# Attention stages with only TensorE held to the written order, and constants set up ahead of an up chunk

## The chip, the cores and the metric

The kernel runs on one core of one Trainium2 chip. The metric is the device time of one execution in microseconds (us), taken as the median over runs. The engines are named as in the profile: PE is TensorE's matmuls, PEld its weight loads, DVE is VectorE, ACT is ScalarE, POOL is GpSimd, SP is SyncE, which issues most DMAs (SPq is its queue). L12 is line 12 of the kernel's source.

## The reference, cut to what matters

One sequence of 256 tokens of width 1024 goes through two stacks of two layers each. All arithmetic is fp32.

```
for l in range(2):                                     # first stack
    x = x + 0.5 * swiglu(rms_norm(x, g1[l]), ...)
    x = x + hybrid_mixer(rms_norm(x, gm[l]), ...)      # NSA (compressed + selected + window) and MoBA heads
    x = x + 0.5 * swiglu(rms_norm(x, g2[l]), ...)
x = rms_norm(x, norm_final)
for l in range(2):                                     # second stack
    h = rms_norm(x, attn_norm[l]);  proj = h @ w_in[l]
    ya = sparse_attention(...)      # 8 heads, each query keeps 64 keys chosen by an index score
    yb = rms_norm(diff_attention(...), b_subln[l])     # 4 heads: softmax 1 - lambda * softmax 2
    x = x + (sigmoid(g_a) * (ya @ w_up_a) + sigmoid(g_b) * (yb @ w_up_b)) @ w_out[l]
    x = x + (silu(h2 @ w_gate) * (h2 @ w_up)) @ w_ffn_out[l]
```

## The kernel before

**Stages.** The program is ten stages in a row: FFN, mixer, FFN, FFN, mixer, FFN (the first stack), then hybrid, FFN, hybrid, FFN. In the profiled execution the mixers run from 204 to 384 us and from 759 to 941 us, the hybrids from 1128 to 1371 us and from 1556 to 1793 us. Here they are called the four attention stages.

**Weights.** A full fp32 product is made of three passes over rounded halves: hi by hi, hi by lo, lo by hi. So every block of weights that lands from a DMA in a buffer `raw` is split in two steps: ACT copies it to `hi` (L189 in the FFN, L1586 in the attention stages), then DVE subtracts to make `lo` (L190, L1587). A half block is 128x1024. There are 3 `raw`, 4 `hi` and 4 `lo` buffers, and 4 accumulator banks `acc` in PSUM beside the banks `psS` (two), `psT` and `psO` (one each).

**Attention stages.** The big products of such a stage (projections L210 to L212, output or up projections) are work that can be put anywhere. A planner (`Fill`, L1595ff) lays them out in program order between the steps of the attention: `fill.us(t)` puts t us of matmuls there, and with them, in program text, the splits of weights that come next (`Fill.split`, by the progress of the product that is running). The attention itself is a row of slots (12 in a mixer, 8 in a hybrid, `pipeline`). In each slot PE makes the scores of two heads (L429 to L433). For each of the two heads and two blocks of queries DVE takes the negative maximum `nm` (L437) and ACT the exponential `P` (L440). DVE forms a coefficient `c` (L640 and L641, L634 with a gate; L1184 in a hybrid) and scales P by it (L479, L480). PE transposes P (L452, L453, L458), ACT copies the greater part of it out of PSUM as `PT` (L454), DVE the rest (L459), and PE multiplies it with the values (L494, L496; L1286 for differential heads). ACT and DVE then split the output (`oh`, `ol`; L223, L224). A slot's own fill lies between the transposes and the values, the scores of the next slot between those.

Other places of the mixer that matter here: `kt`, the transposed keys of the second kind (copied by DVE, L625), ahead of the scores of slot 1; the compressed branch's probabilities, also on DVE ahead of that (L890 to L903); the compression of keys and values, whose weights `ck` and `cv` are fetched by SP (L175, L800) and multiplied at L811; its GELU chain (L834 to L837) ahead of L842 and L858. In a hybrid the rope norm (DVE L1009, which needs POOL's L1002 and its root `hr`, L204) comes ahead of the first slot; the gates `ma` are made by DVE (L1215) and ACT (L1221).

**What sets the order.** From L707 in the mixer and L1375 in the hybrid a stage is under `tc.manual_schedule(engines=MANUAL)`, until its last slot and product are written. Engines in MANUAL execute in the order of the program text there. Elsewhere, and on engines outside MANUAL, a scheduler at build time picks from what is ready, and takes what stands first in the text.

**The first stage.** `ffn` runs over chunks c of 512 columns (L334): gate product, its evacuation (`total`, L327) and SiLU into `sgs`, then up product, whose banks come from psS, psT and psO, and its evacuation. In the first FFN alone a function `extra` makes constants (PE L138, L141, L960 into three acc banks, DVE `gcol` L139 and others behind them, then sine and cosine tables for the second stack). It is bound by `issue_after` to come after the latest product and weight split.

Of the kernel before, what the change touches and what calls it, by code (L numbers as in the profile page):

```python
# [14 lines left out]
ALU = mybir.AluOpType  # L15
AX = mybir.AxisListType
ENG = mybir.EngineType
MANUAL = {ENG.PE, ENG.Activation, ENG.DVE, ENG.Pool}
PSUM = bass.MemoryType.PSUM

DEPTH = 2
# [13 lines left out]
class K:  # L35
# [256 lines left out]
    def ffn(self, pr, wg, wu, wd, scale, after, start=None, load=None, extra=None):  # L292
        nc, tc = self.nc, self.tc
        xx = pr.xx
        self.n_ft = -1
        with tc.tile_pool(name="ffn", bufs=2) as fp:
            gh = fp.tile([128, NF, S], F32R, name="gh", bufs=1)
            gl = fp.tile([128, NF, S], F32R, name="gl", bufs=1)

            def product(w, c, n, banks, first):  # L300

                cs = slice(c * 512, c * 512 + n * 128)
                for h in range(2):
                    src = w[h * 512 : (h + 1) * 512, cs].rearrange("(k p) f -> p k f", p=128)
                    if first and h == 0:
                        hi, lo = start(lambda: self.weights(src, [4, n * 128], 2))
                    else:
                        hi, lo = self.weights(src, [4, n * 128])
                    for j in range(n):
                        fs = slice(j * 128, (j + 1) * 128)  # L310
                        for k in range(4):
                            xk = xx[:, 4 * h + k]
                            nc.tensor.matmul(  # L313
                                banks[j], hi[:, k, fs], xk.rearrange("p u s -> p (u s)"),
                                start=h == 0 and k == 0, stop=False,
                            )
                            self.last = nc.tensor.matmul(  # L317
                                banks[j][:, 0:S], lo[:, k, fs], xk[:, 0, :],
                                start=False, stop=h == 1 and k == 3,
                            )  # L320

            def total(bank, name):

                low = fp.tile([128, S], F32, tag="low", name="low")
                nc.scalar.copy(low, bank[:, S : 2 * S])
                v = fp.tile([128, S], F32, tag=name, name=name, bufs=5)
                nc.vector.tensor_tensor(v, bank[:, 0:S], low, op=ALU.add)  # L327
                return v

            for c in range((NF + 3) // 4):  # L330
                n = min(4, NF - 4 * c)
                banks = [self.acc() for j in range(n)]
                product(wg, c, n, banks, start is not None and c == 0)
                if c == 0:  # L334
                    pr.finish()
                    if load is not None:
                        load()
                    pr.broadcast()
                sgs = []
                for j in range(n):  # L340
                    g = total(banks[j], "g")
                    nc.gpsimd.tensor_tensor(g, g, pr.rbc, op=ALU.mult)  # L342
                    th = fp.tile([128, S], F32, name="th")
                    nc.scalar.activation(th, g, AF.Tanh, scale=0.5)  # L344
                    nc.vector.scalar_tensor_tensor(g, th, 1.0, g, op0=ALU.add, op1=ALU.mult)  # L345
                    sgs.append(g)
                banks = [self.ft() for j in range(n)]
                product(wu, c, n, banks, False)
                for j in range(n):
                    f = 4 * c + j  # L350
                    u = total(banks[j], "u")
                    nc.gpsimd.tensor_tensor(sgs[j], sgs[j], pr.rbc, op=ALU.mult)  # L352
                    hh = fp.tile([128, S], F32, name="hh")
                    nc.gpsimd.tensor_tensor(hh, sgs[j], u, op=ALU.mult)  # L354
                    self.split(gh[:, f, :], gl[:, f, :], hh)
                if extra is not None and c == 2:
                    extra()
            self.to_residual(
                lambda k: gh[:, k, :], lambda k: gl[:, k, :], wd, NF, 0.5 * scale, after
            )  # L360
# [192 lines left out]
    def mixer(self, l, pr, after):  # L553
# [3 lines left out]
        with tc.tile_pool(name="mix", bufs=1) as mp, ExitStack() as es:  # L557
# [40 lines left out]
            def rope2(src):  # L598
                s4 = src.rearrange("p t (g d) -> p t g d", g=2)
                self.rope_part(mp, s4, s4, 2)  # L600
# [105 lines left out]
            next(comp)  # L706
            es.enter_context(tc.manual_schedule(engines=MANUAL))  # L707
            rope2(kv[:, :, 256:384])
# [304 lines left out]
    def hybrid(self, l, pr, after):  # L1013
# [3 lines left out]
        with tc.tile_pool(name="hyb", bufs=1) as mp, ExitStack() as es:  # L1017
# [356 lines left out]
            fill.prime()  # L1374
            es.enter_context(tc.manual_schedule(engines=MANUAL))  # L1375
            fill.later(8.0, pr.broadcast)
# [348 lines left out]
```

## Time and profile before

| | us |
|---|---|
| three runs | 1992.40, 1993.37, 1989.26 |
| median | 1992.4 |
| the profiled execution's own time | 1992.76 |
| its span in the trace | 1991.0 |
| PE busy | 1850.7 |
| DVE busy | 1322.6 |
| ACT busy | 1004.0 |
| POOL busy | 581.4 |

The own time is what was measured around the profiled execution; the span is from its first to its last instruction, 1.76 us less. The granted clock of PE, averaged over the span, is 0.969 of full speed. In a view of waits a line "PE psS L429 <- DVE kt L625: 4.4, 1, 4.4" says that PE stood at L429 for psS until DVE's L625 had written kt: total, number of times, longest. In a timeline an entry in square brackets gives the engine's idle time ahead of the instruction, and what ended it.

### The profile page before, as it was taken

Reading aid. Unit: us, or ns where it says so; the run is one execution under the profiler, and the core shown is the slowest. Engines: PE = TensorE matmul, PEld = TensorE weight load, DVE = VectorE, ACT = ScalarE, POOL = GpSimd, SP = SyncE. Lnnn points to the kernel's source line nnn. Section 1 sums busy time; section 2 is a strip of 40 time slices with the busy share of each in tenths; the row PEclk is TensorE's granted clock in tenths of the full one; section 3 lists DMA queues with packets and bytes.
Section 4 is the critical chain, followed back from the end, with each engine's and each line's share of the span. In section 5 each row is a group of like instructions: output and inputs, shape, how many; then the busy total and the mean of one; then the engine's idle time right before and its main releaser. Section 6 shows DMA issues by size and latency. Waiting matters only on the chain.

```text
span 1991.0 us, 27090 instructions
## 1 busy us (share of the span) xinstructions
PE 1850.7 (93%) x10136; PEld 1540.6 (77%) x10136; DVE 1322.6 (66%) x2202; ACT 1004.0 (50%) x1948; POOL 581.4 (29%) x628
## 2 busy tenths in 40 slices
PE   8899878899999999788999998799999997899999
PEld 6788756688888877556888876697887785888887
DVE  6765555677667665456876588657766697568763
ACT  6554434655555554245655444546555444546552
POOL 5441100055315421000454144001542261014540
PEclk9899989999999999799999999999999998999999
DMA  7546422555655464323555544236546443255543
GB/s 260 186 142 233 162 87 57 173 173 157 233 169 177 154 241 131 125 64 107 189 170 183 182 138 148 85 108 210 170 150 233 152 148 101 91 180 179 180 159 126
DMA packets 149075, 314.40 MB, mean 158 GB/s; under 512 B 5588, under 2 KB 30320, under 8 KB 148944
## 3 DMA queue, kind: packets, MB, share of 16 engines
q1 hardware_dynamic: 148016, 311.15, 47.4%
q0 software_dynamic: 896, 1.52, 0.3%
q8 instruction: 79, 1.29, 0.3%
q14 instruction: 52, 0.43, 0.1%
q10 hardware_dynamic: 32, 0.01, 0.0%
HBM read 311.61 MB, written 1.05 MB: 157 GB/s over the span
## 4 chain that ended last, share of the span: by engine, by line
PE 52%; DVE 20%; ACT 12%; POOL 7%; issue 6%; DMA 2%; SPq 0%; ACTq 0%; POOLq 0%; DVEq 0%
PE acc L253 7%; PE acc L257 7%; PE acc L252 7%; PE acc L313 6%; DVE lo L190 6%; DVE lo L1587 4%; ACT P L440 3%; ACT hi L189 3%; PE acc L317 3%; PE psS L313 3%; POOL hh L354 2%; PE acc L210 2%; POOL g L342 2%; PE acc L212 2%; PE acc L211 2%
## 5 line engine op out<-in xcount | busy, mean ns | idle before, releaser
L190 DVE TENSOR_TENSOR lo<-raw,hi 128x1024 fp32r<-128x1024 f32 (+2 forms) x436 | 535.1, 1254 | 156.6 <-ACT hi L189 152.2
L189 ACT ACTIVATE hi<-raw 128x1024 fp32r<-128x1024 f32 (+2 forms) x436 | 423.6, 1000 | 147.8 <-PE acc L257 99.0
L313 PE MATMUL acc<-xx,hi 128*128 128x512 f32 x1056 | 375.6, 400 | 9.1 <-DVE gcol L139 6.3
L317 PE MATMUL acc<-xx,lo 128*128 128x256 f32 x1056 | 293.8, 280 | 0.0
L1587 DVE TENSOR_TENSOR lo<-raw,hi 128x1024 fp32r<-128x1024 f32 (+1 forms) x168 | 209.4, 1257 | 61.3 <-ACT hi L1586 61.2
L313 PEld LDWEIGHTS acc<-xx,hi 128*128 128x128 f32 x1056 | 199.5, 190 | 57.1 <-DVE gcol L139 6.6
L253 PE MATMUL acc<-lo,gh 128*128 128x512 f32 x528 | 209.3, 396 | 2.7 <-DVE lo L190 2.7
L252 PE MATMUL acc<-hi,gh 128*128 128x512 f32 x528 | 210.0, 398 | 0.0
L317 PEld LDWEIGHTS acc<-xx,lo 128*128 128x128 f32 x1056 | 200.5, 190 | 1.2
L313 PE MATMUL psS<-xx,hi 128*128 128x512 f32 x528 | 192.6, 398 | 2.2 <-ACT hi L189 2.2
L342 POOL TENSOR_TENSOR g<-g,rbc 128x256 f32<-128x256 f32 x132 | 135.0, 1036 | 178.6 <-DVE g L327 128.0
L354 POOL TENSOR_TENSOR hh<-g,u 128x256 f32<-128x256 f32 x132 | 138.2, 1054 | 162.2 <-DVE u L327 161.5
L257 PE MATMUL acc<-hi,gl 128*128 128x512 f32 x528 | 173.8, 396 | 0.0
L210 PE MATMUL acc<-hi,xx 128*128 128x512 f32 (+2 forms) x416 | 170.4, 410 | 1.6 <-ACT xx L1523 1.6
L1586 ACT ACTIVATE hi<-raw 128x1024 fp32r<-128x1024 f32 (+1 forms) x168 | 168.4, 1037 | 4.3 <-PE acc L212 4.3
L212 PE MATMUL acc<-hi,xx 128*128 128x512 f32 (+2 forms) x416 | 161.8, 389 | 2.1 <-DVE xx L1524 2.1
L211 PE MATMUL acc<-lo,xx 128*128 128x512 f32 (+2 forms) x416 | 161.5, 389 | 1.8 <-DVE lo L1587 1.8
L352 POOL TENSOR_TENSOR g<-g,rbc 128x256 f32<-128x256 f32 x132 | 134.7, 1025 | 66.1 <-DVE g L345 66.1
L317 PE MATMUL psS<-xx,lo 128*128 128x256 f32 x528 | 148.6, 282 | 3.9 <-DVE lo L190 3.9
L223 ACT ACTIVATE gh<-hh 128x256 fp32r<-128x256 f32 x132 | 55.4, 420 | 172.0 <-POOL hh L354 171.6
L344 ACT ACTIVATE th<-g 128x256 f32<-128x256 f32 x132 | 55.1, 419 | 152.6 <-POOL g L342 152.3
L345 DVE SCALAR_TENSOR_TENSOR g<-th,g 128x256 f32<-128x256 f32 x132 | 82.5, 629 | 73.6 <-ACT th L344 73.6
(431 smaller groups left out, 3678.4 us busy)
## 6 DMA issues: line engine op xcount, KB each, us to landing
raw<-in_w_in_dram SPq DMA_DIRECT2D x60, 1024.0 KB, 5.1
raw<-in_w_ffn_down_dram SPq DMA_DIRECT2D x44, 1024.0 KB, 5.0
raw<-in_w_ffn_up_dram SPq DMA_DIRECT2D x40, 1024.0 KB, 5.2
raw<-in_w_ffn_in_dram SPq DMA_DIRECT2D x40, 1024.0 KB, 5.2
raw<-in_w_ffn_gate_dram SPq DMA_DIRECT2D x39, 1024.0 KB, 5.1
raw<-in_w_ffn_out_dram SPq DMA_DIRECT2D x22, 1024.0 KB, 5.0
raw<-in_w_out_dram SPq DMA_DIRECT2D x12, 1024.0 KB, 4.9
raw<-in_w_ffn_gate_dram SPq DMA_DIRECT2D x10, 512.0 KB, 3.8
```

What stands on the lines that cost most here:

```text
L189: nc.scalar.activation(hi[:, hs], raw[:, hs], AF.Copy),
L190: nc.vector.tensor_tensor(lo[:, hs], raw[:, hs], hi[:, hs].bitcast(F32), op=ALU.subtract),
L210: mm(out, ah, bh, start=start, stop=False)
L211: mm(out, ah, bl, start=False, stop=False)
L212: self.last = mm(out, al, bh, start=False, stop=stop)
L252: mm(accs[t, n], ah, hi[:, j, cs], start=k == 0, stop=False)
L253: mm(accs[t, n], ah, lo[:, j, cs], start=False, stop=False)
L257: mm(accs[t, n], al, hi[:, j, cs], start=False, stop=k == nk - 1)
L313: nc.tensor.matmul(banks[j], hi[:, k, fs], xk.rearrange("p u s -> p (u s)"), start=h == 0 and k == 0, stop=False,)
L317: self.last = nc.tensor.matmul(banks[j][:, 0:S], lo[:, k, fs], xk[:, 0, :], start=False, stop=h == 1 and k == 3,)
L354: nc.gpsimd.tensor_tensor(hh, sgs[j], u, op=ALU.mult)
L1587: nc.vector.tensor_tensor(self.lo[:, hs], self.raw[:, hs], self.hi[:, hs].bitcast(F32), op=ALU.subtract)
```

## The change

Two edits. MANUAL shrinks from four engines to PE alone, so in the attention stages ACT, DVE and POOL are ordered by the scheduler, among what is ready by place in the text. And `extra()` moves from behind the third up chunk (c == 2) of the first FFN to ahead of that chunk's up product.

```
-MANUAL = {ENG.PE, ENG.Activation, ENG.DVE, ENG.Pool}
+MANUAL = {ENG.PE}
...
                     sgs.append(g)
+                if extra is not None and c == 2:
+                    extra()
                 banks = [self.ft() for j in range(n)]
                 product(wu, c, n, banks, False)
                 for j in range(n):
...
                     self.split(gh[:, f, :], gl[:, f, :], hh)
-                if extra is not None and c == 2:
-                    extra()
             self.to_residual(
```

PE's order in the attention stages stays as it is. In the first stage L138, L141 and L960 move from behind the third up product to ahead of it; on DVE the small constants ahead of them (L125 to L953, eight operations or so) come one chunk earlier, and `gcol` and what follows stand behind the third of that chunk's four gate evacuations. On SP the fetch of `ck` for the values' half of the mixer is issued ahead of that of `cv`, where it stood behind it.

The three fences below show the order of one engine at a place, first before and then after. A number behind a name tells one buffer of that name from another.

DVE in the first mixer, from the maxima `nm` of slot 0 to the copy of `kt` (e, ec and pc belong to the compressed branch). Before:

```order
L437 TENSOR_REDUCE nm_2445<-psS_2448 128x1 x2
L1587 TENSOR_TENSOR lo_2469<-raw_2277,hi_2468 128x1024
L890 TENSOR_TENSOR e_2438<-e_2438,cvalid_930 128x256
L894 TENSOR_REDUCE ec_2482<-e_2438 128x16
L895 TENSOR_SCALAR ec_2482<-ec_2482 128x16
L896 RECIPROCAL ec_2482<-ec_2482 128x16
L902 TENSOR_TENSOR ec_2482<-ec_2482,gt_2093 128x8
L903 TENSOR_TENSOR pc_2486<-e_2438,ec_2482 128x8x16
L902 TENSOR_TENSOR ec_2482<-ec_2482,gt_2093 128x8
L903 TENSOR_TENSOR pc_2486<-e_2438,ec_2482 128x8x16
L625 COPY kt_2495<-psT_2492 128x256
```

After:

```order
L890 TENSOR_TENSOR e_2438<-e_2438,cvalid_810 128x256
L894 TENSOR_REDUCE ec_2482<-e_2438 128x16
L437 TENSOR_REDUCE nm_2445<-psS_2447 128x1
L437 TENSOR_REDUCE nm_2445<-psS_2448 128x1
L895 TENSOR_SCALAR ec_2482<-ec_2482 128x16
L896 RECIPROCAL ec_2482<-ec_2482 128x16
L625 COPY kt_2495<-psT_2492 128x256
L902 TENSOR_TENSOR ec_2482<-ec_2482,gt_2093 128x8 x2
```

The split of `lo_2469` has left the place, the four operations on ec and pc have gone behind `kt`, and the maxima of the two banks psS_2447 and psS_2448 take turns.

ACT in a slot of the first mixer (before, the one at 298 to 303 us), from the split output `oh` to the copy `PT_2684`. Before:

```order
L223 ACTIVATE oh_2007<-psO_2534 128x256
L440 ACTIVATE P_2650,sm_2652<-psS_2653,nm_2651 128x256
L440 ACTIVATE P_2650,sm_2652<-psS_2653,nm_2651 128x128
L440 ACTIVATE P_2650,sm_2652<-psS_2654,nm_2651 128x256
L440 ACTIVATE P_2650,sm_2652<-psS_2654,nm_2651 128x128
L1586 ACTIVATE hi_2678<-raw_2466 128x1024
L454 COPY PT_2684<-psT_2683 128x2x256
```

After:

```order
L1586 ACTIVATE hi_2770<-raw_2558 128x1024 x2
L223 ACTIVATE oh_2007<-psO_2534 128x256
L440 ACTIVATE P_2650,sm_2652<-psS_2653,nm_2651 128x256
L440 ACTIVATE P_2650,sm_2652<-psS_2654,nm_2651 128x256
L454 COPY PT_2684<-psT_2683 128x2x256
L440 ACTIVATE P_2650,sm_2652<-psS_2653,nm_2651 128x128
```

The copy of `PT` has moved ahead of a split and of two exponentials, and the split that now stands near it is that of a later block (hi_2770 in place of hi_2678). On DVE in the same slot, before:

```order
L224 TENSOR_TENSOR ol_2008<-psO_2534,oh_2007 128x256
L437 TENSOR_REDUCE nm_2651<-psS_2653 128x1 x2
L437 TENSOR_REDUCE nm_2651<-psS_2654 128x1 x2
L1587 TENSOR_TENSOR lo_2679<-raw_2466,hi_2678 128x1024
L459 COPY PT_2684<-psO_2682 128x2x128
```

After:

```order
L1587 TENSOR_TENSOR lo_2771<-raw_2558,hi_2770 128x1024
L224 TENSOR_TENSOR ol_2008<-psO_2534,oh_2007 128x256
L1587 TENSOR_TENSOR lo_2771<-raw_2558,hi_2770 128x1024
L437 TENSOR_REDUCE nm_2651<-psS_2653 128x1
L437 TENSOR_REDUCE nm_2651<-psS_2654 128x1
```

Here the split between the maxima and the copy `PT` is gone, and two splits of a later block stand around `ol`, ahead of the maxima.

ACT in a slot of the first hybrid (before, the one at 1283 to 1291 us), at the gates `ma` and the copy `PT_11408`. Before:

```order
L440 ACTIVATE P_11361,sm_11363<-psS_11365,nm_11362 128x128
L1586 ACTIVATE hi_11338<-raw_11076 128x1024
L1221 ACTIVATE ma_10151<-ma_10151,hbias_915 128x256 x4
L454 COPY PT_11408<-psT_11407 128x2x256
L223 ACTIVATE yah_10149<-psO_11406 128x256
```

After:

```order
L1586 ACTIVATE hi_11559<-raw_11336 128x1024
L440 ACTIVATE P_11361,sm_11363<-psS_11365,nm_11362 128x128
L1221 ACTIVATE ma_10151<-ma_10151,hbias_795 128x256 x2
L454 COPY PT_11408<-psT_11407 128x2x256
L1586 ACTIVATE hi_11559<-raw_11336 128x1024
L223 ACTIVATE yah_10149<-psO_11406 128x256
```

Two of the four gates have gone a slot up, and a half of a later block stands on each side of the copy.

## Rows read from the trace of the kernel before

**Rows 1.** The page's first lines: the span, and each engine's busy time, share of the span and instructions.

```profile
span 1991.0 us, 27090 instructions
...
PE 1850.7 (93%) x10136; PEld 1540.6 (77%) x10136; DVE 1322.6 (66%) x2202; ACT 1004.0 (50%) x1948; POOL 581.4 (29%) x628
```

**Rows 2.** Busy time by stage: the stretch, its length, then busy time (and instructions) of PE, PEld, DVE, ACT and POOL, PE's granted clock, the DMA engines' busy share and GB/s. First mixer, the FFN behind it, second mixer, the two hybrids.

```profile
204.00:384.00 180.00, 150.86 (x859) 113.83 (x857) 99.94 (x235) 78.23 (x189) 16.54 (x33) 0.93 0.34 104
384.00:571.00 187.00, 184.96 (x972) 156.27 (x972) 131.06 (x181) 101.83 (x183) 69.58 (x69) 1.00 0.58 194
...
759.00:941.00 182.00, 153.35 (x856) 115.97 (x855) 99.30 (x234) 77.53 (x189) 14.98 (x31) 0.92 0.31 95
...
1128.00:1371.00 243.00, 214.34 (x1284) 182.35 (x1283) 171.17 (x318) 119.72 (x241) 60.29 (x60) 0.94 0.40 133
...
1556.00:1793.00 237.00, 212.21 (x1285) 181.12 (x1284) 167.93 (x313) 117.04 (x232) 60.34 (x55) 0.95 0.40 133
```

**Rows 3.** What PE waited for in the first mixer, 204 to 384 us: total, times, longest. ("issue" is a wait that the profile shows no releaser of.)

```profile
PE psO L494 <- DVE c L640: 5.1, 2, 3.0
PE psS L429 <- DVE kt L625: 4.4, 1, 4.4
PE psS L811 <- DMA raw<-in_w_ck_dram: 4.3, 1, 4.3
PE psS L842 <- issue: 3.2, 1, 3.2
PE psT L458 <- ACT PT L454: 2.7, 4, 1.1
PE acc L252 <- ACT hi L1586: 2.5, 2, 1.3
PE acc L253 <- DVE lo L1587: 1.5, 2, 0.8
PE psO L496 <- DVE PT L459: 1.5, 1, 1.5
...
PE psS L858 <- issue: 1.4, 1, 1.4
```

**Rows 4.** The same view of the first hybrid, 1128 to 1371 us.

```profile
PE psS L429 <- ACT P L440: 7.0, 1, 7.0
PE psO L494 <- ACT PT L454: 4.8, 1, 4.8
PE psO L1286 <- DVE c L1184: 4.8, 2, 2.4
PE acc L252 <- ACT hi L1586: 2.2, 1, 2.2
...
PE acc L211 <- DVE lo L1587: 0.8, 2, 0.6
```

**Rows 5.** Timeline of SP's queue in the first mixer: start, duration, the DMA.

```profile
236.34 0.50 SPq L800 DMA_DIRECT2D cv<-in_w_cv_dram  x1
236.90 1.86 SPq L175 DMA_DIRECT2D raw<-in_w_ck_dram  x1
```

**Rows 6.** Timeline of DVE in the first mixer at `kt`: start, duration, instruction, idle time ahead of it.

```profile
273.66 1.23 DVE L1587 TENSOR_TENSOR lo<-raw,hi 128x1024 fp32r<-128x1024 f32 x1 [1.47 <-ACT hi L1586]
274.80 0.42 DVE L890 TENSOR_TENSOR e<-e,cvalid 128x256 f32<-128x256 f32 x1
...
277.09 0.42 DVE L625 COPY kt<-psT 128x256 f32<-128x256 f32 x1
```

**Rows 7.** Timeline of ACT in a slot of the first mixer.

```profile
300.97 1.05 ACT L1586 ACTIVATE hi<-raw 128x1024 fp32r<-128x1024 f32 x1
301.92 0.57 ACT L454 COPY PT<-psT 128x512 f32<-128x512 f32 x1
```

**Rows 8.** Timeline of DVE in the same slot.

```profile
302.05 1.23 DVE L1587 TENSOR_TENSOR lo<-raw,hi 128x1024 fp32r<-128x1024 f32 x1 [1.47 <-ACT hi L1586]
303.19 0.42 DVE L459 COPY PT<-psO 128x256 f32<-128x256 f32 x1
```

**Rows 9.** Timeline of ACT in a slot of the first hybrid.

```profile
1289.01 1.71 ACT L1221 ACTIVATE ma<-ma,hbias 128x256 f32<-128x256 f32 x4 [1.89 <-DVE ma L1215]
1290.63 0.56 ACT L454 COPY PT<-psT 128x512 f32<-128x512 f32 x1
```

**Rows 10.** Timeline ahead of the first slot of the first hybrid: the same rope operation of DVE twice, and a POOL operation beside the first.

```profile
1231.99 1.75 DVE L1009 TENSOR_TENSOR xk<-t,hr 128x512 f32<-128x512 f32 x1 [1.05 <-POOL hr L204]
...
1235.86 0.68 DVE L1009 TENSOR_TENSOR xk<-t,hr 128x512 f32<-128x512 f32 x1
...
1231.92 1.27 POOL L993 TENSOR_TENSOR t<-xk,tab 128x512 f32<-128x512 f32 x1
```

**Rows 11.** Two short stretches, columns as in rows 2: one in the first mixer right around the end of the wait for `kt`, one in the first stage behind `extra`.

```profile
276.09:282.92 6.83, 5.26 (x19) 4.33 (x20) 5.00 (x17) 1.72 (x7) 0.00 (x0) 0.52 0.45 147
...
88.35:98.59 10.24, 5.86 (x18) 4.98 (x19) 9.05 (x27) 4.41 (x10) 3.00 (x4) 0.52 0.50 157
```

**Rows 12.** What PE waited for longest in the first stage, 0 to 204 us: total, times, longest.

```profile
PE acc L313 <- DVE gcol L139: 6.3, 1, 6.3
```

**Rows 13.** Timeline of the first stage at chunk c == 2: the first matmul of its up product on PE, and DVE's evacuation of the third gate bank.

```profile
72.96 0.40 PE L313 MATMUL psS<-xx,hi 128*128 128x512 f32 x1
...
79.55 0.41 DVE L327 TENSOR_TENSOR g<-acc,low 128x256 f32<-128x256 f32 x1
```

More of the change, by code (lines that the diff above doesn't have):

```diff
@@ L17 @@
 ENG = mybir.EngineType
-MANUAL = {ENG.PE, ENG.Activation, ENG.DVE, ENG.Pool}
+MANUAL = {ENG.PE}
 PSUM = bass.MemoryType.PSUM
@@ L346, in ffn @@
                     sgs.append(g)
+                if extra is not None and c == 2:
+                    extra()
                 banks = [self.ft() for j in range(n)]
@@ L355, in ffn @@
                     self.split(gh[:, f, :], gl[:, f, :], hh)
-                if extra is not None and c == 2:
-                    extra()
             self.to_residual(
```

## The prediction

> **What bounds the kernel now.** I read the page's busy times first: PE works 1850.7 of 1991.0 us and DVE, next, 66% [rows 1], so PE's idle 140 us are the most that an edit of order can touch, apart from the clock. The stretches by stage say where they lie: an FFN leaves PE idle for 2 of 187 us, a mixer for 29.1 (180 less 150.86) and 28.7, a hybrid for 28.7 and 24.8 [rows 2]. So 111 us of the idle time lie in the four stages that the first edit touches. In the same rows PE's clock is 1.00 in the FFN and 0.92 to 0.95 in these stages: at 0.93, 7% of the mixer's 150.86 us of PE work, some 10.6 us, is time that the half clock adds, and 6% of 214.34, 12.9 us, in a hybrid [rows 2]. The views of PE's waits then name what ends the idle time. Most of it is not DVE or ACT being full, but a copy that PE needs standing behind something that PE does not need yet [rows 3, 4]. That is what an order can change.
>
> **The sum.** It is made against the profiled execution's own 1992.76 us (span 1991.0 and 1.76 around it); the median of the three runs is 0.36 lower. The twin stages are alike in length, idle time and clock, so each is worked out once and doubled.
>
> *A mixer.* (1) `ck`: PE waits 4.3 us for its DMA [rows 3], which SP issues 0.56 us behind that of `cv` [rows 5]; now it goes first, and the three buffers `raw` come free sooner, since the narrow splits stand earlier on DVE. I take all of it, +4.3 (bounds 0 and 4.3). (2) `kt`: 4.4 us [rows 3]. DVE stood idle for 1.47 us and split for 1.14 more before L890, and `kt` began 2.29 us behind that [rows 6]. By the order the split is gone from there, and four of the eight small operations go behind `kt`: 2.61 and some 0.9, +3.5 (2.6 to 4.4). (3) The copies `PT`: L494 and L496 wait 6.6 us [rows 3]. In the slot shown ACT's copy began at 301.92, straight behind a split of 1.05 [rows 7]; DVE's began at 303.19, behind 1.47 of idleness and a split of 1.23 [rows 8]. ACT's copy now comes ahead of the split, and DVE's has none straight ahead of it. I take +4.5 (0 to 6.6), since the maxima still stand ahead. (4) L458 waits for psT until ACT's copy has read it, 2.7 [rows 3]; the same move gives about half, +1.5 (0 to 2.7). (5) L252 and L253 wait for weights, 4.0 [rows 3]. The splits run one block ahead of where the text puts them, so +4.0 (0 to 4.0). (6) In the GELU chain that L842 and L858 wait for (3.2 and 1.4, [rows 3]) the scheduler has put halves of splits: two of them, of which I count 0.85 each as not hidden, -1.7 (0 to -2.5, two splits of 1.23). (7) The clock: the stretch around the wait for `kt` ran at 0.52 [rows 11], so that its 5.26 us of PE work were some 2.6 longer than at full clock. If the wait is gone the cause that the row shows, an idle engine, is gone too. I take +4 of the 10.6 (0 to 10.6). (8) New waits. Splits that run ahead of the text stand in front of something: in the slot shown two of them around `ol`, ahead of the maxima. The maxima are not what PE waits for next (a slot of fill and a transposition lie between), so most are hidden; a split of 1.23 [rows 8] in one of two slots is -8 (0 to -15, one in each of 12). Sum: 4.3 + 3.5 + 4.5 + 1.5 + 4.0 - 1.7 + 4 - 8 = 12.1, twice 24.2.
>
> *A hybrid.* (1) L494 and L1286 wait 9.6 us for `PT` and `c` [rows 4]. In the slot shown ACT's copy stands behind 1.89 us of idleness and four gates of 1.71 [rows 9]; now two of the gates are a slot earlier and two are still in front. +6.5 (0 to 9.6). (2) Weights, 2.2 and 0.8 [rows 4]: +3.0 (0 to 3.0). (3) The clock: +4 of 12.9 (0 to 12.9). (4) The first slot's 7.0 us [rows 4]: DVE reaches the maxima late because rope and splits fill it; the number of splits ahead of them hardly changes (some 28 before and 30 after, over both places in the text), so 0 (-5, four splits, to +3). (5) New waits, as in a mixer, in four of eight slots: -5 (0 to -10). Sum: 6.5 + 3.0 + 4 + 0 - 5 = 8.5, twice 17.0.
>
> *The first stage.* The 6.3 us that PE waits for the bank that `gcol` is read from [rows 12] go, and so may part of the half clock behind them (0.52 over 10.24 us, [rows 11]). In their place PE, which began the up product at 72.96, must first transpose into three acc banks that the gate evacuation frees; the third of those was read from 79.55 for 0.41 [rows 13], so PE stands for up to 7.0 us at L960. Eight small constants of DVE are no longer ahead of that evacuation, which brings some 1.5 back. It is one wait for another: 0 (-1 to +3). What stands behind on DVE, `gcol` and seven more, is small against the up product that follows, which hides it; with that cover gone it would be about 1 us.
>
> Total: 24.2 + 17.0 + 0 = 41.2, and 1992.76 - 41.2 = 1951.6, by the median's footing **1951 us**. The FFN stages between keep PE 99% busy and are not counted.
>
> **A collision that the order may bring.** DVE's rope operation L1009 took 1.75 us while POOL ran L993 beside it for 1.27, and 0.68 the next time [rows 10]: 1.07 us for a meeting. The Trainium skill ("SBUF — State Buffer", Who interferes with whom) says that a DVE instruction with two SBUF inputs and a GpSimd instruction that reads SBUF share one read interface, and that the later one is blocked entirely. By that rule, with which these rows agree, each split that the scheduler drops between POOL's rope operations may block either engine.
>
> **The rivals.**
>
> A. *Splits ahead of what PE needs, in each slot* (slower). Without the new waits the gains are 20.1 in a mixer and 13.5 in a hybrid, 67.2 in all. There are 40 slots. If the splits cost more than 67.2 / 40 = 1.68 us in each, the change loses. The row that speaks for it is the order itself: two splits stand ahead of the maxima in the slot shown, 2.46 us, and if they delay `PT` in full everywhere, it is 98 us: 1992.8 - 67.2 + 98.4 = **2024**. Against it: before, DVE sat idle for 1.47 us in that very slot waiting for ACT [rows 8], and only 100 of a mixer's 180 us are busy there [rows 2], so a split ahead of time falls into idle time.
>
> B. *No gain, since one wait takes the other's place.* The two engines have the same work, and a hybrid's DVE is busy for 171 of 243 us [rows 2]. If each removed wait uncovers the next in line within the same slot, it stays at **1992**. Against it: of rows 3 and 4 the greatest are single events, not one in each slot.
>
> C. *POOL and DVE collide ahead of the hybrid's first slot.* There the 7.0 us wait hangs on rope and `hr`; five more meetings of 1.07 [rows 10] make it 5.4 longer, 10.7 in both hybrids: **1962**. For it: splits there have moved, and POOL's own order too. Against: before, splits stood among these operations as well.
>
> D. *The clock comes back as well.* If new waits stay at half of my terms and the clock gives back about two thirds of 10.6 and 12.9, that is 4 + 3 more in a mixer and 2.5 + 4.6 in a hybrid, 28 in all: **1923**. For it: the half clock lies right at the waits that go [rows 11].
>
> That the change doesn't do what it says is ruled out by the order: all three free engines stand otherwise than in the text.
>
> **How the numbers follow.** Forecast 0.55, A 0.16, B 0.07, C 0.10, D 0.12. A change of 0.2% (4 us) is about what a measurement of this kernel can tell from none. Faster: 0.55 + 0.10 + 0.12 = 0.77; same 0.07 (B); slower 0.16 (A). If every bound fell well (mixer 32.6, hybrid 25.5, twice) it would be 1992.8 - 116 = 1877, which I do not expect; the range goes from 1915, a little under D, to 1995, with B in and A out: it holds about 8 in 10.
>
> **What would show it.** Right: in a mixer the waits for `ck` and `kt` gone or under 1 us, the longest for `PT` under 1.5, the clock at 0.95 or more, a mixer some 12 us shorter and a hybrid some 8. The FFNs unchanged within 1 us. In the first stage a wait of 4 to 7 us at L138 to L960 in place of that at L313. Wrong: many small waits of about 1.2 us for `PT`, `c` or P in nearly each slot, with a split ahead of them on DVE or ACT (A); the wait ahead of a hybrid's first slot at 10 or more (C); a stage of attention as long as before with new releasers (B). The forecast falls also if the transition to the next FFN, where the two orders mix PE's work otherwise, costs more than 2 or 3 us each.

## The result, and the profile after

The changed kernel takes 1891.4 us (median of four runs, 1890.8 to 1894.9) against 1992.5 before (also four): a ratio of 0.950, 95% interval 0.948 to 0.952. That is 101 us less, where 41 were forecast and 1915 was the low end of the range. The page of the changed kernel, first lines, beside [rows 1]:

```profile
span 1889.4 us, 27118 instructions
...
PE 1809.0 (96%) x10136; PEld 1519.8 (80%) x10136; DVE 1314.4 (70%) x2202; ACT 998.1 (53%) x1948; POOL 596.3 (32%) x628
```

The 101.6 us by which the span fell are 59.9 us of idle PE (140.3 before, 80.4 now) and 41.7 us of PE's own busy time, for the same 10136 matmuls. PE's mean granted clock rose from 0.969 to 0.984: 0.031 x 1991.0 less 0.016 x 1889.4, or 31 of those 42 us, is the clock by this reading. The clock's own records say the same: PE was busy for 104 us inside the stretches at the lower of its two levels (1.2 GHz, half of 2.4) before and for 43 us now, and half of that, 52 and 21 us, is what the level cost.

For the stages I cut both spans at the same event, the last residual addition of a stage. Busy time by stage, columns as in [rows 2]; both mixers and both hybrids before, then the same after:

```profile
212.54:389.22 176.68, 146.74 (x838) 110.25 (x836) 100.74 (x230) 76.66 (x183) 16.54 (x33) 0.93 0.37 114
...
767.45:946.77 179.32, 149.86 (x838) 112.74 (x836) 100.73 (x230) 76.68 (x183) 14.98 (x31) 0.91 0.34 106
...
1138.42:1375.52 237.10, 208.44 (x1256) 177.82 (x1255) 169.64 (x312) 115.66 (x231) 59.55 (x60) 0.94 0.41 136
...
1566.85:1797.89 231.04, 206.25 (x1256) 176.53 (x1255) 166.44 (x308) 113.12 (x223) 59.60 (x55) 0.95 0.42 137
```

```profile
212.68:356.08 143.40, 137.08 (x838) 105.70 (x837) 99.51 (x232) 75.24 (x183) 24.00 (x33) 0.98 0.46 145
...
732.99:877.08 144.09, 137.57 (x838) 106.35 (x837) 99.61 (x232) 75.17 (x183) 21.48 (x29) 0.98 0.44 136
...
1067.30:1288.44 221.14, 199.96 (x1253) 173.13 (x1252) 167.49 (x313) 114.78 (x231) 61.90 (x60) 0.96 0.44 146
...
1478.60:1697.68 219.08, 198.76 (x1253) 172.54 (x1252) 166.40 (x309) 112.39 (x223) 61.36 (x55) 0.96 0.44 145
```

The mixers are 33.3 and 35.2 us shorter (12.1 forecast), the hybrids 16.0 and 12.0 (8.5 forecast). An FFN behind one of them is 1.2 to 1.5 us shorter, the first stage and the other FFN the same within 0.2. In the first mixer idle PE fell from 29.9 to 6.3 us and PE's busy time by 9.7. DVE and ACT do the same work in it, so it is the order alone. What PE still waits for there, 204 to 384 us, all of it, beside [rows 3]:

```profile
PE psS L842 <- issue: 3.5, 1, 3.5
PE psS L429 <- DVE mkT L417: 1.3, 1, 1.3
PE psS L858 <- issue: 1.1, 1, 1.1
PE psO L494 <- DVE PT L459: 0.3, 1, 0.3
```

The waits for `ck`, `kt`, the weights and L458 are gone, those for `PT` and `c` are down to 0.3. No new wait took their place. At `kt`, DVE's timeline beside [rows 6]: it copies `kt` 0.8 us after it had nothing left to do, as soon as PE has transposed it.

```profile
265.41 0.25 DVE L896 RECIPROCAL ec<-ec 128x16 f32<-128x16 f32 x1
266.45 0.42 DVE L625 COPY kt<-psT 128x256 f32<-128x256 f32 x1 [0.79 <-PE psT L623]
```

The slot of [rows 7] and [rows 8] now, ACT first, then DVE:

```profile
284.14 0.47 ACT L440 ACTIVATE P<-psS,nm 128x256 f32<-128x256 f32 x1
...
284.58 0.58 ACT L454 COPY PT<-psT 128x512 f32<-128x512 f32 x1
```

```profile
280.10 1.47 DVE L1587 TENSOR_TENSOR lo<-raw,hi 128x1024 fp32r<-128x1024 f32 x1
281.49 0.41 DVE L224 TENSOR_TENSOR ol<-psO,oh 128x256 fp32r<-128x256 f32 x1
281.82 1.42 DVE L1587 TENSOR_TENSOR lo<-raw,hi 128x1024 fp32r<-128x1024 f32 x1
283.17 0.74 DVE L437 TENSOR_REDUCE nm<-psS 128x1 f32<-128x256 f32 x2
...
284.93 0.41 DVE L459 COPY PT<-psO 128x256 f32<-128x256 f32 x1
```

PE's first matmul with that slot's `PT`, before and then now:

```profile
303.76 1.12 PE L494 MATMUL psO<-PT,kv 128*64 128x256 f32 x4 [3.00 <-DVE c L640]
```

```profile
285.49 0.65 PE L494 MATMUL psO<-PT,kv 128*64 128x256 f32 x4 [0.27 <-DVE PT L459]
```

The two splits stand ahead of the maxima, as the order had said, and PE waits 0.27 us in this slot, where it waited 3.00 in the old order. They fill time in which DVE has nothing that PE is waiting for. The old order left DVE idle for 1.47 us in the same place, waiting for ACT's half of the split.

The hybrids gained less. The longest waits in the first of them, beside [rows 4]; behind them DVE ahead of its first slot, beside [rows 10]:

```profile
PE psS L429 <- ACT P L440: 10.1, 1, 10.1
PE psS L1114 <- DVE ikd L1009: 3.7, 2, 3.4
PE psT L1320 <- DVE ybl L1324: 1.8, 1, 1.8
PE psO L494 <- DVE PT L459: 1.2, 1, 1.2
...
PE psO L494 <- ACT PT L454: 0.7, 1, 0.7
```

```profile
1162.38 1.76 DVE L1009 TENSOR_TENSOR xk<-t,hr 128x512 f32<-128x512 f32 x1 [2.81 <-POOL hr L204]
1164.06 1.21 DVE L1587 TENSOR_TENSOR lo<-raw,hi 128x1024 fp32r<-128x1024 f32 x1
...
1165.80 2.35 DVE L1587 TENSOR_TENSOR lo<-raw,hi 128x1024 fp32r<-128x1024 f32 x2
...
1168.67 1.21 DVE L1587 TENSOR_TENSOR lo<-raw,hi 128x1024 fp32r<-128x1024 f32 x1
1169.80 0.75 DVE L437 TENSOR_REDUCE nm<-psS 128x1 f32<-128x256 f32 x2
```

`PT` and `c` went from 9.6 to 1.9 us, but the wait for the first slot's P grew from 7.0 to 10.1 and one for the index key (L1114) is new: DVE stands for 2.81 us at L1009 (1.05 before) until POOL has made `hr`, and between there and the maxima come four splits, where there were two before.

The first stage has the wait that was forecast, in place of the 6.3 us of [rows 12]:

```profile
PE acc L138 <- DVE g L327: 3.9, 1, 3.9
...
PE acc L960 <- DVE g L327: 1.3, 1, 1.3
```

### The profile page after: what moved, and what is told of

It is laid out like the page before. It is cut to its first block, busy times and chain, and to the rows that moved or that the text cites. A ratio compares the mean times of both kernels' runs of the same rounds, so it can differ in the third digit from the quotient of the medians.

```text
span 1889.4 us, 27118 instructions
## 1 busy us (share of the span) xinstructions
PE 1809.0 (96%) x10136; PEld 1519.8 (80%) x10136; DVE 1314.4 (70%) x2202; ACT 998.1 (53%) x1948; POOL 596.3 (32%) x628
## 3 DMA queue, kind: packets, MB, share of 16 engines
HBM read 311.61 MB, written 1.05 MB: 165 GB/s over the span
## 4 chain that ended last, share of the span: by engine, by line
PE 68%; DVE 14%; POOL 7%; ACT 6%; issue 4%; DMA 1%; ACTq 0%; POOLq 0%; DVEq 0%
PE acc L313 9%; PE acc L257 8%; PE acc L253 8%; PE acc L252 8%; PE acc L317 5%; PE psS L313 4%; DVE lo L1587 4%; DVE lo L190 3%; PE acc L210 3%; PE acc L211 3%; PE acc L212 3%; PE psT L313 2%; PE psS L317 2%; PE psO L313 2%; POOL hh L356 2%
## 5 line engine op out<-in xcount | busy, mean ns | idle before, releaser
L313 PE MATMUL acc<-xx,hi 128*128 128x512 f32 x1056 | 370.6, 396 | 0.0
```

Source lines behind the costliest of these rows:

```text
L313: nc.tensor.matmul(banks[j], hi[:, k, fs], xk.rearrange("p u s -> p (u s)"), start=h == 0 and k == 0, stop=False,)
```

## The experiments

Times are medians of four runs (e2: ten); "gain" is against the kernel before, measured beside them on the same chip. Three theories were at stake: **place** (splits leave the places that the text gives them ahead of PT, c, kt and P, and run ahead), **turns** (the maxima and exponentials of two heads alternate, so DVE and ACT don't wait for each other four times a slot), and **one engine** (DVE's order, or ACT's, alone).

**The two edits apart.**

```
 e1   MANUAL = {ENG.PE}, extra() in its old place
 e2   MANUAL = {ENG.PE, ENG.Activation, ENG.DVE, ENG.Pool}, extra() in its new place
```

> Only the first edit: in the attention stages PE alone is held to the text, the constants stay behind the third up chunk. If the move of the constants is worth nothing, as its term of 0 had it and as the first stage's end (212.54 and 212.68 us) reads: 1891 us, within 4 of the changed kernel, with the 6.3 us wait for gcol back and the 3.9 and 1.3 us waits at L138 and L960 gone. If the move carries part of the gain, more than 5 us above 1891.

> Only the second edit, all four engines held as before. If it is worth nothing: 1992 us, within 4 of the kernel before. If setting constants up sooner helps later stages: 1985 or less.

e1: 1893.4, ratio 0.950 (0.948 to 0.952). e2: 1993.0, ratio 1.000 (0.999 to 1.002). The gain is the first edit's alone.

**One engine held.**

```
-MANUAL = {ENG.PE}
+MANUAL = {ENG.PE, ENG.Activation}      # e3;  e4: {ENG.PE, ENG.DVE}
```

> The changed kernel with ACT held to the text again in the attention stages, DVE and POOL free. Theory 'place' (the gain is that splits of weights leave the places that the text gives them ahead of PT, c, kt and P, and a split is two steps on two engines): DVE cannot run its step ahead of ACT's, ACT's copies of PT stand behind its splits again, so 50 to 85 of the 101 us come back, 1941 to 1976. Rival 'DVE alone' (the waits named DVE's c, kt, PT and lo most often): under 25 come back, 1916 or less.

> The changed kernel with DVE held to the text again, ACT and POOL free. Theory 'place': ACT's step runs ahead, DVE's split still stands ahead of c, PT and kt but no longer waits 1.47 us for ACT there, so 25 to 60 of the 101 us come back, 1916 to 1951. Rival 'ACT alone' (what counts is that the copy PT stands ahead of the last exponentials): under 20 come back, 1911 or less.

e3: 1955.1, gain 38. e4: 1946.3, gain 47. Either engine held gives back more than half, and both times lie where "place" had them, so neither engine is enough. The two runs do not part "place" from "turns": an engine held to the text has its maxima, or its exponentials, in the old order as well. The first mixer of e3, waits of PE:

```profile
PE psS L811 <- DMA raw<-in_w_ck_dram: 4.4, 1, 4.4
PE acc L252 <- ACT hi L1586: 3.5, 2, 1.8
PE psO L494 <- ACT PT L454: 3.4, 5, 1.2
```

Waits for `PT` come back, and the whole wait for `ck`; e4 has that too (4.3). A buffer `raw` is free only when both steps of its split are done, so one engine in text order holds up SP's fetches.

**Turns by text.** The kernel before, all held, the loops over heads and query blocks exchanged:

```
-        for i, b in enumerate(ps):
-            for t, c0, c1 in ((0, 0, 256), (1, 256, 384)):
+        for t, c0, c1 in ((0, 0, 256), (1, 256, 384)):
+            for i, b in enumerate(ps):
```

> The kernel before, all four engines held to the text, but the text takes the maxima and exponentials of the two heads in turn (as the scheduler does), not one head after the other. Rival 'turns' (the shorter chain from maxima to P is what gains): most of the 101 us, 1945 or less. Theory 'place': P is rarely what PE waits for (13.9 of 140 us idle, in the hybrids' first slot), so 1975 to 1992.

1955.4, ratio 0.982 (0.980 to 0.984), gain 35: between the two expectations. "Place" had taken P for something PE hardly waits for, but P's last exponential is what `PT`, `c` and the split on ACT queue behind. With the same splits at the same places, PE's waits for `PT` and `c` (L494, L496, L1286 and L458 in the view of the whole span) fall from 38.6 to 23.7 us, so the four hand-overs of a slot count.

**Splits kept out of a part of the slot.** The planner writes no coming split between `turn()` and `values()` (e6); the same with the turns (e7).

```
-            if self.i + 1 < len(self.items):
+            if self.i + 1 < len(self.items) and not self.hold:
...
+            fill.hold = True
             rest = turn()
...
             values()
+            fill.hold = False
```

> The kernel before, all four engines held, but the planner writes no split of the coming weights between a slot's transposes and its values; what it holds back comes behind the values. Theory 'place': the waits for PT, c and P weighing in the slots (some 38 us) go for the greater part and the half clock at them too, 1940 to 1965; the waits for weights (18 us) and ck (8) stay or grow. Rival 'turns': 1985 or more. Rival 'ahead' (what gains is that splits run ahead of the text, so weights and buffers come sooner): 1990 or more, since splits only come later here.

> Both of these edits by hand in the kernel before, all four engines held. If place and turns are the whole of it, 1900 to 1930. If running ahead (ck, weights, kt) makes a part of its own, it stops short of the changed kernel by at least the 35 us of those waits: 1930 to 1960.

e6: 2015.1, 24 us slower than before; e7: 1977.1, gain 14 and 22 less than with the turns alone. Both miss what "place" expected, and e6 lies where the two rivals had it (turns 1985 or more, splits that come later 1990 or more). But the edit did not do what I meant. What it held back came out behind the values, in the text still ahead of the next slot's `PT`. ACT, then DVE, in a slot of e6:

```profile
299.66 1.04 ACT L1588 ACTIVATE hi<-raw 128x1024 fp32r<-128x1024 f32 x1
300.61 0.57 ACT L454 COPY PT<-psT 128x512 f32<-128x512 f32 x1
```

```profile
300.74 1.22 DVE L1589 TENSOR_TENSOR lo<-raw,hi 128x1024 fp32r<-128x1024 f32 x1 [1.47 <-ACT hi L1588]
301.88 0.42 DVE L459 COPY PT<-psO 128x256 f32<-128x256 f32 x1
```

That is the picture of [rows 7] and [rows 8], now in more slots: of the 40 copies `PT` that ACT makes, 12 come straight behind a split in the kernel before, 28 in e6 and 2 in the changed kernel. PE's waits for `PT` and `c` grow with that from 38.6 to 54.7 us, while those for weights stay (18.3 and 18.5) and those for `ck` hardly change (8.2 and 9.0). So what e6 loses comes from the place of the splits, not from weights that come later: a test of "place" with the sign turned round. It also shows how hard a good fixed place is to write by hand.

**How much a slot hides.** The changed kernel with each maximum taken twice:

```
+                for _ in range(2):
                     nc.vector.tensor_reduce(nm[:, j : j + 1], b[:, c0:c1], axis=AX.X, op=ALU.max, negate=True)
```

> The changed kernel with each maximum taken twice (the second overwrites the first with the same): four more DVE operations in each of 40 slots, 2 x 0.42 + 2 x 0.29 = 1.42 us, 57 us of DVE in all, right at the place where the prediction feared the splits. If slots have slack there (which would be why new waits came to nothing): under 15 us more, 1906 or less. If each us ahead of P is paid by PE, as rival A of the prediction had it: 57 us and the half clock at the new waits, 1948 or more.

1915.4, 24 us more than the changed kernel and between the two expectations. The 57 us were too high. The page of e8 has 160 more operations on DVE and 39.6 us more of busy time than that of the changed kernel (1314.4):

```profile
PE 1815.7 (95%) x10136; PEld 1521.6 (80%) x10136; DVE 1354.0 (71%) x2362; ACT 998.4 (52%) x1948; POOL 597.0 (31%) x628
```

So some 40% of what was added there is hidden and 60% is paid. A slot has a little slack at its maxima, but not much.

**Only the splits free.** e9: PE and POOL held, and each DVE and ACT call in an attention stage tied behind the one before it in the text, except in `Chunk.half`, which makes the splits. e10: the same with the turns.

```
-MANUAL = {ENG.PE}
+MANUAL = {ENG.PE, ENG.Pool}
...
+            r = f(*args, **kw)                    # any nc.vector or nc.scalar call
+            if k.pin and hasattr(r, "ins"):
+                k.tc.add_manual_dep(r.ins, k.prev[key].name, NoSync, ...)
+                k.prev[key] = r.ins
...
+        was, k.pin = k.pin, False                 # Chunk.half
         nc.scalar.activation(self.hi[:, hs], self.raw[:, hs], AF.Copy)
         nc.vector.tensor_tensor(self.lo[:, hs], ...)
+        k.pin = was
```

> Attention stages with PE and POOL held to the text and every DVE and ACT instruction chained in the order of the text, except the splits of weights, which the scheduler may put anywhere. Theory 'two parts' (turns, 36 us by the run with the turns written by hand, and free splits, the rest): 1925 to 1935, with the waits for ck and weights gone and the waits for c and PT smaller. If free splits are nearly all of it, 1905 or less; if other moved operations (kt ahead of the small ones, PT ahead of the last P) carry the rest, 1950 or more.

> The same with the turns of maxima and exponentials in the text. Theory 'two parts': 1888 to 1900, the changed kernel's time. If the other moved operations count: 1908 or more.

e9: 1933.1, ratio 0.970 (0.968 to 0.971), gain 60. e10: 1896.0, ratio 0.951 (0.949 to 0.953), gain 97. Both as "two parts" had it: 60 and 35 make 95, and with both by hand only 4 us are missing to the changed kernel. Those 4 us are a net figure. By the same cut e10's mixers are 9.3 and 5.3 us longer than the changed kernel's (152.7 and 149.4), and its hybrids 3.8 and 7.2 shorter (217.3 and 211.9).

What the freed splits gain by themselves is read from PE's waits. The first mixer of e9, beside [rows 3] (L494 and L458 are L534 and L498 there, and L47 is the helper that ties the calls):

```profile
PE psO L534 <- ACT PT L47: 5.0, 5, 1.5
...
PE psT L498 <- ACT PT L47: 4.5, 4, 1.5
```

The waits for `ck` and for weights, 8.3 us, are gone. Those for `PT` and `c` are 9.5 us, about what they were (9.3 in [rows 3]): few splits stand straight ahead of `PT` now, but some have gone between the exponentials of a slot. Over the whole span PE's waits for weights and `ck` go from 26.5 to 0 us (one of 1.2 for `cv` is new), those for `PT` and `c` only from 38.6 to 32.6, and to 12.3 in e10. So the 60 us come mostly from splits that run ahead, and the waits for `PT` go when the turns come too.

**All free, without the turns.** The loop of e5's diff in its old form, inside a region of its own:

```
+        with self.tc.manual_schedule(engines={ENG.DVE, ENG.Activation}):
+            for i, b in enumerate(ps): ...
```

> The changed kernel with the four maxima and four exponentials of a slot tied in the old order, one head after the other; all else free. If the turns are worth the same 36 us here as alone: 1921 to 1933. If the free splits already take out what the turns gain (the slots then have slack): 1905 or less.

1906.0, gain 87, a little above the second expectation. The turns are worth 35 us alone, 37 on top of free splits (e9 to e10) and 14 here. So the turns do not overlap with the free splits, but with the freedom of all the other operations (`PT`, `c`, `kt`, those of POOL). That freedom is worth 27 us without the turns (e9 to e11) and 4 with them (e10 to the changed kernel).

**The hybrids' front.** Held on all four engines until the first slot's scores (e12), or with DVE and ACT chained in text order except the splits (e16, which also has the loops of e5); free from there. The code is that of e12.

```
-            es.enter_context(tc.manual_schedule(engines=MANUAL))
+            held.enter_context(tc.manual_schedule(engines={ENG.PE, ENG.Activation, ENG.DVE, ENG.Pool}))
...
             fill.until("bv")
+            held.close()
+            es.enter_context(tc.manual_schedule(engines=MANUAL))
             slots = [diff(h) for h in range(4)] + [sparse(k) for k in range(4)]
```

> The changed kernel with all four engines held in the hybrids up to the first slot's scores, as before, and free from there. The waits ahead of the second scores are 15.5 and 14.1 us in the changed kernel's hybrids and 10.5 and 7.7 before; if the free order of that part is to blame for the difference, 11 us and a little clock come back: 1876 to 1884. If the early part pays for the later slots by splits made ahead of time there: 1889 or more.

> Mixers all free; hybrids with DVE and ACT chained in the order of the text up to the first slot, except the splits, and all free from there. In the run with splits free and turns the hybrids took 217.3 and 211.9 us, with the front held 218.4 and 213.8, all free 221.1 and 219.1. If only the splits' freedom is good in the front: 1875 to 1882. If the chained slots were what made the difference: 1884 or more.

e12: 1883.0, gain 110. e16: 1882.0, gain 110. Both as expected: in the front the order of the text is better than the free one, by 8 to 10 us.

**The price of one wait.** The changed kernel with each copy of `kt` made 6 times (e13) or 13 times (e14).

```
+                    for _ in range(6):
                         nc.vector.tensor_copy(kt, pst[:, 0:256])
```

> The changed kernel with each copy of kt made six times over (the last five overwrite it with the same), so that kt comes some 2.1 us later at the two places of each mixer. What does a wait of PE cost in all, with its half clock? If the half clock is bound to long waits only: a wait of at most 2 us a mixer appears, no new stretch at half clock, and the time is the wait, 1891 to 1896. If any wait brings it: 1898 or more.

> The same with each copy made 13 times, some 5 us later (and other DVE work put between). If the half clock follows the long wait, as before beside the 4.4 us wait for kt (6.83 us at 0.52): a wait of 3 to 6 us in each mixer and one more stretch of 3 to 7 us at half clock, so each costs its wait and 1 to 3 us more: 1898 to 1911. If the clock had other causes (the share of DVE or ACT work, the order as such): the wait alone, no new stretch, 1897 to 1903 at most.

e13: 1913.2; e14: 1928.6: 22 and 37 us more than the changed kernel. e13 lies where any wait brings the half clock (1898 or more), but its waits are of 3.8 and 4.8 us, not of 2. e14 is above both of its ranges, since each mixer has two such places, of which I had counted one, and the waits are longer than the 3 to 6 us that I took. The first mixer of e14, waits, and two stretches around them and one behind (columns as in [rows 2]):

```profile
PE psS L429 <- DVE kt L626: 8.5, 1, 8.5
PE psT L411 <- DVE kt L626: 7.0, 1, 7.0
```

```profile
246.62:253.45 6.83, 3.95 (x18) 3.98 (x19) 3.23 (x7) 0.60 (x1) 0.74 (x1) 0.50 0.48 172
280.76:287.59 6.83, 3.63 (x14) 3.09 (x15) 3.98 (x12) 1.07 (x5) 0.00 (x0) 0.50 0.70 152
290.00:330.00 40.00, 39.72 (x253) 29.68 (x252) 28.51 (x75) 23.02 (x66) 7.70 (x8) 1.00 0.24 80
```

Each long wait has its stretch of half clock, and 40 us of dense slots have none. The mixers of e14 are longer than the changed kernel's by 17.4 and 18.2 us (160.8 and 162.3 by the same cut), with 14.4 and 13.7 us more of idle PE; the rest, 3 to 4.5 us, is PE running slower.

**The waits that are left.** e15: on e12, 5 us of projection ahead of the compression's last step. e17: on that, 9 us in place of 2.8 between a hybrid's first two scores. e18: both on e16.

```
             fill.until("kw")
+            fill.us(5.0)
             next(comp, None)
...
-        fill.us(2.8)                              # pipeline(), behind the first scores
+        fill.us(f0)                               # f0 = 9.0 in the hybrids, 2.8 in the mixers
```

> The version with the hybrids' front held (1883), and in the mixers 5 us more of projection put between the planner's 'until kw' and the last step of the compression, where PE waits 3.5 and 1.2 us for the GELU chain with 6.83 us of half clock behind it. If that wait and its clock are all that is left: 1883 less 2 x 6 to 7, 1869 to 1873. If the work that goes there is missed in a later slot: 1879 or more.

> The version of e15 with 9 us in place of 2.8 of projection between the first and the second scores of a hybrid, where PE waits 9.1 and 9.0 us for P with 13.7 us of half clock in each hybrid. If the wait is for want of work of PE's alone: 5 to 6 us of each wait and some clock go, 1853 to 1859. If DVE is what is short there (the fill needs splits, which stand ahead of the maxima): the wait only moves, 1866 or more.

> The same two edits on the version of e16 (front chained, its splits free), whose wait there is 6.2 us. If the wait is for want of PE's work: 1852 to 1860. If DVE is what is short: 1866 or more.

e15: 1869.7, gain 122. e17: 1855.3, gain 136. e18: 1850.2, ratio 0.929 (0.928 to 0.930), gain 141: the best of all, 2.2% below the changed kernel. The expectations that saw PE short of work held; e18 is 2 us under its range. The first mixer of e15 as one stretch; and the longest wait of e15 in the whole span, then the same line in e17:

```profile
213.00:351.00 138.00, 135.75 (x840) 104.34 (x839) 101.14 (x233) 74.78 (x185) 23.37 (x32) 1.00 0.51 158
```

```profile
PE psS L429 <- ACT P L440: 18.1, 2, 9.1
```

```profile
PE psS L429 <- ACT P L440: 2.1, 2, 1.0
```

With the last long wait gone the mixer runs at full clock throughout.

## Why the prediction was wrong

**The reading of the bound held.** The time lay in the four attention stages, in copies that stood behind something that PE did not need yet, and the order was what could move it.

**Mixer, terms 1 to 5** (17.8 us): right in kind, somewhat small. `ck` gave 4.3 (taken 4.3), `kt` 4.4 (3.5), `PT` and `c` 6.3 (4.5), L458 2.7 (1.5), the weights 4.0 (4.0): 21.7. I had kept part of the `PT` waits because the maxima still stood ahead; the turns took that part too, which I had seen in the order and given no term. The forecast's upper bounds were also added up too low: with the +3 of the hybrid's term 4 and the +3 of the first stage, which it left out, the 1877 would be 1868.

**Mixer, term 6** (-1.7): 4.6 us of waits at L842 and L858 before and 4.6 after. The splits that the order puts into the chain do not show.

**Mixer, term 8, new waits (-8): the first step that failed.** Nothing of it came: 0.3 us in a slot with two splits ahead of its maxima. I took splits in front of the maxima for half exposed. They run in time that DVE had been idle: the slot shown waits 0.27 us with both of them there. It is not that DVE has time to spare right at the maxima, since of the work that e8 adds there some 60% is paid. Rival A, which made the same fear into a loss, had the evidence against it in its own text, the 1.47 us idle of [rows 8], and I did not carry that over into the term.

**Mixer and hybrid, term 7 and term 3, the clock (16 us of gain in all): the second step that failed.** PE's busy time fell by 9.7 and 12.3 us in the mixers, 8.5 and 7.5 in the hybrids, and 41.7 in all, of which 31 are the clock. By the clock's records the half clock had cost 10.6 and 14.2 us in the mixers and 11.0 and 10.0 in the hybrids, near the 10.6 and 12.9 of the forecast; 2.3, 3.1, 4.9 and 5.7 of that are left. So two thirds of it went, 30 us in these four stages, where I had taken about a third as an overall share. [Rows 11] tied such a stretch to one wait, and e13 to e15 confirm it: put two long waits in, and two stretches come; take the last one out, and the clock is 1.00. So the term had to be read wait by wait: if the waits for `ck`, `kt` and `PT` go, their stretches go with them.

**Hybrid, waits** (4.5 us net of new ones forecast, 7.5 and 4.5 measured): right in sum, with some luck, since the parts are off in ways that cancel. `PT` and `c` gave 7.7 (6.5). The first slot's wait, held at 0, cost 3.1. Rival C had its sign; its price was for collisions between POOL and DVE, whereas the rows show a longer wait on POOL's `hr` and four splits in place of two, with the meeting at L1009 as long as before (1.76 and 1.75). The front as a whole costs 8 to 10 us by e12 and e16.

**First stage** (0): right, with the wait of 5.2 us in place of 6.3 as forecast, and e2 at 1.000.

**In sum**, the forecast fell 60 us short. Of that, 26 is PE's busy time (16 forecast, 41.7 measured): 15 the clock, and 10 shorter work that the clock does not explain. In the mixers 16 is new waits that did not come, 8 the waits that I took in part, 3 term 6, and 3 small waits that had no term. The hybrids' waits make 3, and the other stages 1. Rival D had the mechanism of the clock term and was given 0.12.

What is shown and what is argued: that freed splits (60 us) and turns (35) together bring the whole to within 4 us (a net figure, as said above), and that either engine held gives back more than half, is shown by runs. That the free splits gain mostly by running ahead is read from the waits of e9; no run lets them run ahead without leaving their places. That 31 of the 42 us of PE's busy time are the clock is arithmetic on the granted clock; where the other 10 went is open. POOL was never freed or held alone, so its part is open.

## What to carry to other kernels

A wait of the bounding engine costs more than its length if its clock falls with it: pair each stretch at half clock with the wait beside it, and let the two go or stay together in the sum. An operation that runs ahead costs little where its engine was idle (0.27 us for two splits in the slot shown), so look at the idle time ahead of it before pricing it as a new wait. And where a two-step job (ACT, then DVE) is placed by hand, freeing one engine is not half of freeing both; a front in which text order is better can still be held by itself.

## What the runs showed of the hardware that was not expected

The clock's price for a wait: in the change, 59.9 us less waiting made the kernel 101.6 us faster, a factor of 1.7 (with the 10 us in it that the clock does not explain), where the dosed waits of e14 give 28.1 us of idle time for 35.6 us of mixer, a factor of 1.3. In the first mixer of e13 the 3.8 us wait had 3.4 us at half clock beside it and the 4.8 us wait 6.8; in that of e14 waits of 7.0 and 8.5 us had 6.8 each. The second mixers have 6.8 beside waits of 3.8 and 3.7 us, and 10.2 and 6.8 beside 7.0 and 7.9. So in these runs a longer wait did not cost more clock in proportion. The first mixer of before had waits of 4.3, 3.2, 4.4, 3.0 and 2.1 us, 17.0 in all, with 23.9 us at half clock; that of e14 had 19.0 us in four waits, of 7.0, 2.1, 1.3 and 8.5, with 17.1. Nor did each wait have its stretch: two of 2.4 us in the hybrids of before had none. Two such stretches of e13's first mixer, where the clock is at its lower level:

```profile
245.10:248.50 3.40, 3.40 (x17) 3.40 (x16) 0.69 (x1) 1.31 (x2) 0.73 (x1) 0.50 0.87 324
272.40:279.20 6.80, 4.48 (x16) 3.71 (x17) 4.37 (x13) 1.84 (x8) 0.00 (x0) 0.50 0.60 130
```
